# Hybrid encoder trunk, out-projection and first up chunk: GpSimd's sums and splits moved to VectorE, operands traced just ahead of their products, the token factors' transposes three products later

## The chip, the cores and the metric

The kernel runs on one core of a Trainium2 chip. The metric is the device time of one execution in microseconds; the time quoted is the median of several executions. TensorE multiplies matrices, VectorE and ScalarE work element by element, GpSimd is the fourth compute engine, SyncE issues most of the transfers. The engines run beside one another and wait for each other at semaphores.

## What is computed

Two layers. Each takes x (1024 tokens of 1024 features), mixes tokens in three parallel head groups, projects back and adds, and then runs a gated feed-forward network with a depthwise convolution of width 3 on the gate:

```python
mix = jnp.concatenate([o_a, o_b.astype(x.dtype), o_c], axis=-1)
x = x + mix @ w_out[l].astype(x.dtype)

hf = rms_norm(x, ffn_norm[l]) @ w_up[l].astype(x.dtype)
gate, val = hf[..., :D_FF], hf[..., D_FF:]
gate = depthwise_conv(gate, conv_w[l], conv_b[l])
x = x + (jax.nn.gelu(gate, approximate=False) * val) @ w_down[l].astype(x.dtype)
```

D_FF is 2816, everything is float32, and the norm is x · rsqrt(mean(x²) + eps) · gain over the features of a token.

## The kernel before

All data stand with features on the partitions and tokens along the row. A float32 product is made of three: each operand is split in a high half (a rounded copy, made by ScalarE) and a low half (the rest, a subtraction), and high·high, high·low and low·high are summed in PSUM. Every split thus costs a ScalarE copy and then a subtraction, on VectorE unless something else is said.

**Out-projection** (`out_proj`, L963 to L1006). A loop over the eight blocks of 128 output features, in the order 0, 4, 1, 5, 2, 6, 3, 7, here called columns. Each column takes 48 matmuls of 128x512 (L269). Then the old x is added (L983, VectorE), the sum `X` stored (L984), squared (ScalarE, L990) and added into a running sum of squares `ssq` (L991): on GpSimd, but for the last column on VectorE. The rest of the column already prepares the feed-forward: for blocks 0 to 3 the difference of the two token halves (`xd`, L997, GpSimd), scaled by the gain (L998), and the split of operand 11; for blocks 4 to 7 the second half of `xd` (L1004) and the split of operand T2. In the seventh column `up_begin` (L1080) traces the weights of the first up chunk.

**Up-projection** (`up`, L1083). 22 chunks, each 128 gate and 128 value features. A chunk is a 2x2 block product (halves of the 1024 inputs, halves of the tokens), made with seven block products instead of eight. `up_weights` loads a chunk's two weight blocks (L1051, L1052, on SyncE's queue) and makes seven weight operands of them (`wo`, splits L1063 and L1064). The seven token operands (`bo`) are the same for all chunks, made once a layer: 11, 21, T2, T1, T3, T4, 22, each of four pieces [high, low] of 128x512, made by `split_x` (L1011); T3 and T4 first need a scaled difference (`xt`, L1096 and L1097; `xd`, L1101). A product is twelve matmuls (L1111). In a chunk they come in the order 0 to 6 by the operands just listed, with product 0 of the next chunk (`begin`, L1122) between the fifth and the sixth. Product 0 and the later ones of a chunk add into one PSUM tile `pa`, and ScalarE copies its stages out: after product 0 (L1126), after T2 (L1139), after T3 (L1146).

**Token factors** (`factors`, L1023). The rsqrt factor of a token is applied behind the products. Eight products of `ssq` with a column of ones (L1028) sum over the features, VectorE and GpSimd make the rsqrt (L190, L195), eight transposes (L1036) spread it over the partitions, and two ScalarE copies (L1037) store it as `rbc`. All of that is called after product T2 of the first chunk.

**What sets the order.** A tile framework deals the traced instructions to each engine in an order of its own: by the order in which the code traces them, by what they wait for, and by its own model of times. Then each engine runs its row strictly in order. Buffers come from rings: 13 slots (`X`, `xd`, `sq`, `v`, `g`, operand 22), 16 for operands 21, T1, T3 and T4, 8 for 11 and T2, 10 for weights, 3 half-width ones (`xt`, one weight sum); PSUM has two tiles each of `pa`, `pb` and `pt`. An instruction that takes a ring's next buffer waits until its last reader is done, on whatever engine that is. In the code before, all of 21, T1, T3, T4 and 22 are traced ahead of product 0, and T1's four low halves are subtracted on GpSimd.

## Time and profile before

| what | value |
|---|---|
| median of 3 executions | 2807.78 us (2807.61 to 2809.55) |
| the profiled execution | 2816.99 us, span 2815.2 us |
| mean granted clock of TensorE | 0.991 of full |
| busy: TensorE, VectorE, ScalarE, GpSimd | 2760.4, 2146.6, 1431.8, 477.3 us |

The profile is of one execution. Its span starts with the first instruction on the device; times of the trace are counted from there. A matmul of 128x512 at the full clock starts 0.2267 us behind the one ahead of it; the trace's duration of a single one is longer, since matmuls overlap. [...] Layer 0's up-projection begins at 774.92, right behind the out-projection; layer 1's at 2171.44.

### The profile page before, as it was taken

Reading aid. Unit: us, or ns where it says so; the run is one execution under the profiler, and the core shown is the slowest. Engines: PE = TensorE matmul, PEld = TensorE weight load, DVE = VectorE, ACT = ScalarE, POOL = GpSimd, SP = SyncE. Lnnn points to the kernel's source line nnn. Section 1 sums busy time; section 2 is a strip of 40 time slices with the busy share of each in tenths; the row PEclk is TensorE's granted clock in tenths of the full one; section 3 lists DMA queues with packets and bytes.
Section 4 is the critical chain, followed back from the end, with each engine's and each line's share of the span. In section 5 each row is a group of like instructions: output and inputs, shape, how many; then the busy total and the mean of one; then the engine's idle time right before and its main releaser. Section 6 shows DMA issues by size and latency. Waiting matters only on the chain.

```text
span 2815.2 us, 39626 instructions
## 1 busy us (share of the span) xinstructions
PE 2760.4 (98%) x14984; PEld 2346.1 (83%) x14984; DVE 2146.6 (76%) x3330; ACT 1431.8 (51%) x2405; POOL 477.3 (17%) x349
## 2 busy tenths in 40 slices
PE   8999999999999999999999999999999999999999
PEld 7999987677878888888899999867778788888887
DVE  5858778798677777788848497788976778778885
ACT  5526367687353344344535264677864444334342
POOL 1202235442310000000002032354323000000000
PEclk9999999999999999999999999999999999999999
DMA  4313362010422222475313033521003122225661
GB/s 152 84 35 103 85 153 72 23 39 8 135 82 68 90 90 73 153 279 157 122 55 87 25 106 96 136 71 46 16 32 134 61 90 89 69 90 197 222 198 64
DMA packets 155200, 273.60 MB, mean 97 GB/s; under 512 B 16769, under 2 KB 74369, under 8 KB 155009
## 3 DMA queue, kind: packets, MB, share of 16 engines
q1 hardware_dynamic: 145216, 241.71, 26.4%
q0 software_dynamic: 9792, 29.36, 4.0%
q8 instruction: 118, 1.93, 0.3%
q14 instruction: 74, 0.60, 0.1%
HBM read 201.80 MB, written 69.21 MB: 96 GB/s over the span
## 4 chain that ended last, share of the span: by engine, by line
PE 87%; DVE 7%; ACT 3%; POOL 1%; issue 1%; DMA 1%; DVEq 0%; SPq 0%; ACTq 0%; POOLq 0%
PE pa L1111 17%; PE pa L281 11%; PE pa L269 11%; PE pb L1111 9%; PE pa L1309 6%; PE pb L860 5%; PE pa L774 5%; PE pt L1309 4%; PE pb L1309 4%; PE pt L1111 4%; PE pt L845 4%; PE pb L619 1%; PE pt L619 1%; DVE ptl L855 1%; PE pt L281 1%
## 5 line engine op out<-in xcount | busy, mean ns | idle before, releaser
L1111 PE MATMUL pa<-bo,wo 128*128 128x512 f32 x2112 | 505.4, 391 | 7.2 <-ACT v L1126 7.2
L1111 PEld LDWEIGHTS pa<-bo,wo 128*128 128x128 f32 x2112 | 398.9, 189 | 91.2 <-ACT v L1126 8.0
L281 PE MATMUL pa<-wh,xh 128*128 128x256 f32 (+1 forms) x864 | 263.6, 306 | 7.9 <-ACT xh L233 7.9
L774 PE MATMUL pa<-qk,qk 96*128 96x512 f32 (+1 forms) x896 | 257.8, 415 | 7.6 <-ACT pa L791 4.2
L281 PE MATMUL pa<-wl,xh 128*128 128x256 f32 (+1 forms) x864 | 262.5, 304 | 2.5 <-DVE wl L336 2.5
L281 PE MATMUL pa<-wh,xl 128*128 128x256 f32 (+1 forms) x864 | 261.4, 304 | 2.5 <-DVE xl L234 2.5
L1111 PE MATMUL pb<-bo,wo 128*128 128x512 f32 x1056 | 253.6, 389 | 0.0
L1111 PEld LDWEIGHTS pb<-bo,wo 128*128 128x128 f32 x1056 | 198.2, 188 | 41.2
L855 DVE TENSOR_TENSOR ptl<-pt,pth 128x512 fp32r<-128x512 f32 x240 | 162.1, 684 | 46.3 <-ACT pth L849 45.0
L1170 ACT ACTIVATE t<-g,pp 128x1024 f32<-128x1024 f32 x44 | 54.8, 1245 | 268.4 <-DVE g L1120 254.7
L774 PEld LDWEIGHTS pa<-qk,qk 96*128 96x128 f32 (+1 forms) x896 | 157.4, 191 | 38.3 <-ACT pa L791 5.1
L849 ACT ACTIVATE pth<-pt 128x512 fp32r<-128x512 f32 x256 | 149.2, 597 | 78.3 <-PE pt L845 74.1
L809 DVE CUSTOM_DVE_ANT_0 pb<-pa,toep 128x1024 f32<-128x1024 f32 x128 | 153.7, 1217 | 29.9 <-PE pa L774 29.5
L1309 PE MATMUL pa<-bw,bw 128*128 128x512 f32 x616 | 174.6, 389 | 0.0
L281 PEld LDWEIGHTS pa<-wh,xh 128*128 128x128 f32 x864 | 166.0, 192 | 8.1 <-ACT xh L233 7.9
L281 PEld LDWEIGHTS pa<-wl,xh 128*128 128x128 f32 x864 | 166.1, 192 | 3.2 <-DVE wl L336 3.0
L281 PEld LDWEIGHTS pa<-wh,xl 128*128 128x128 f32 x864 | 165.3, 192 | 3.4 <-DVE xl L234 3.1
L812 ACT ACTIVATE pb<-pb,nmb 128x1024 f32<-128x1024 f32 x128 | 147.1, 1151 | 36.6 <-DVE nmb L809 35.4
L1063 ACT ACTIVATE wo<-ws 128x512 fp32r<-128x512 f32 x176 | 102.4, 625 | 121.0 <-DVE ws L1059 107.9
L793 POOL TENSOR_SCALAR pa<-pa,z 128x1024 f32<-128x1024 f32 x96 | 110.4, 1150 | 157.8 <-PE pt L845 105.7
L1111 PE MATMUL pt<-bo,wo 128*128 128x512 f32 x528 | 134.7, 390 | 1.8 <-ACT wo L1063 1.8
L1309 PEld LDWEIGHTS pa<-bw,bw 128*128 128x128 f32 x616 | 115.6, 188 | 24.1
(310 smaller groups left out, 6394.2 us busy)
## 6 DMA issues: line engine op xcount, KB each, us to landing
wraw<-w_u SPq DMA_DIRECT2D x88, 512.0 KB, 4.3
hid<-t SPq DMA_DIRECT2D x44, 512.0 KB, 2.9
dq<-hid SPq DMA_DIRECT2D x66, 256.0 KB, 5.1
bk<-st SPq DMA_DIRECT2D x256, 48.0 KB, 1.7
qk<-bk POOLq DMA_DIRECT2D x32, 384.0 KB, 5.0
da<-w_d SPq DMA_DIRECT2D x44, 256.0 KB, 4.8
dp<-w_d SPq DMA_DIRECT2D x44, 256.0 KB, 5.4
dq<-w_d SPq DMA_DIRECT2D x44, 256.0 KB, 4.9
```

The lines of the kernel that those rows point to most:

```text
L269: nc.tensor.matmul(ps[:, hf * 512 : hf * 512 + 512], w, x[:, hf * 512 : hf * 512 + 512], start=first, stop=last)
L281: self.nc.tensor.matmul(ps, x[:, ts], w[:, k % kp, :cols], start=first, stop=last)
L774: nc.tensor.matmul(ps[:, hs], q[:rows, o + t * P : o + (t + 1) * P], kk[w][:rows, hs], start=w == 0, stop=w == 1)
L793: nc.gpsimd.tensor_scalar(e, e, z, 1.0, op0=ALU.mult, op1=ALU.mult)
L809: nc.vector.tensor_tensor_reduce(e, ps, self.toep[:, o : o + T], scale=-slope, scalar=3.0e38, op0=ALU.add, op1=ALU.min, accum_out=nm)
L812: nc.scalar.activation(e, e, AF.Exp, bias=nm, scale=-1.0, accum_out=z[:, t, i : i + 1])
L845: nc.tensor.transpose(ps[:, t * P : (t + 1) * P], Pt[t][:, k * P : (k + 1) * P], self.ident)
L849: nc.scalar.activation(hi[:, kk], ps, AF.Copy)
L855: nc.vector.tensor_tensor(lo[:, kk], ps, hi[:, kk], op=ALU.subtract)
L860: nc.tensor.matmul(acc, s, x, start=k == 0 and j == 0, stop=k == NT - 1 and j == len(ops) - 1)
L1111: nc.tensor.matmul(ps, st, mv, start=first and k + u + v == 0, stop=k == 3 and u == 1, skip_group_check=not first)
L1309: nc.tensor.matmul(acc[j][c], a[u][:, c * P : (c + 1) * P], b[v], start=g == first and q + u + v == 0, stop=q == n - 1 and u == 1, skip_gr ...
```

## The change

The six sums and four differences of a layer go from GpSimd to VectorE, T1's low halves too. The five later operands are traced by a function `build` that the first product of each calls, and T3 ahead of the first add of the chunk. In the first chunk, product 0 is copied to a half-width tile `u1`, and the slots `v` and `g` are taken later. `factors` ends with the rsqrt, and the transposes and copies, now `spread`, are called after product 0 of the second chunk, three products later; both use PSUM tiles `pt`.

```diff
@@ out_proj @@
-                (nc.vector if n == KC - 1 else nc.gpsimd).tensor_tensor(acc, acc, sq, op=ALU.add)
+                nc.vector.tensor_tensor(acc, acc, sq, op=ALU.add)
...
-                nc.gpsimd.tensor_tensor(d[:, 0], X[c][:, 512:], X[c][:, :512], op=ALU.subtract)
+                nc.vector.tensor_tensor(d[:, 0], X[c][:, 512:], X[c][:, :512], op=ALU.subtract)
@@ split_x @@
-            (eng or nc.vector).tensor_tensor(o[:, 1], src, o[:, 0], op=ALU.subtract)
+            nc.vector.tensor_tensor(o[:, 1], src, o[:, 0], op=ALU.subtract)
@@ factors @@
-        ps = self.bank1([P, NT])
+        ps = self.bank1([P, NT], tag="pt")
...
         self.rsqrt(r, ps, D, [NT])
+        return r
+
+    def spread(self, r):
+
+        nc = self.nc
         rbc = self.slot([P, T], name="rbc")
         for hf in range(2):
-            pb = self.bank1([P, 512])
+            pb = self.bank1([P, 512], tag="pt")
@@ up @@
-        for name in ("21", "T1", "T3", "T4", "22"):
+        def build(name):
+
...
-                    o = self.split_x(td[k][:, 0], None, self.xslot, nc.gpsimd)
+                    o = self.split_x(td[k][:, 0], None, self.xslot)
...
+            if (x, 0) not in self.B:
+                build(x)
...
-        def begin():
-
-            v, a = self.slot([P, T], name="v"), self.bank2([P, 512])
+        def begin(u1=None):
+
+
+            v = self.slot([P, T], name="v") if u1 is None else None
+            u1, a = v[:, :512] if u1 is None else u1, self.bank2([P, 512])
             product(0, "11", a)
-            nc.scalar.activation(v[:, :512], a, AF.Copy)
-            return v, a
+            nc.scalar.activation(u1, a, AF.Copy)
+            return v, u1, a
...
-        v, a = begin()
+        v, u1, a = begin(self.half([P, 512], "u1"))
...
-            g, c = self.slot([P, T], name="g"), self.bank1([P, 512], tag="pt")
+            c = self.bank1([P, 512], tag="pt")
             product(1, "21", c)
-            self.mark = [add(v[:, :512], v[:, :512], c)]
+            if f == 0:
+                build("T3")
+                v = self.slot([P, T], name="v")
+            self.mark = [add(v[:, :512], u1, c)]
...
-            if rbc is None:
-                rbc = self.factors(acc)
+            if f == 0:
+                r = self.factors(acc)
...
+            g = self.slot([P, T], name="g")
...
             coming = None if last else begin()
             self.ops = ops + self.ops
+            if f == 0:
+                rbc = self.spread(r)
```

The lines behind it move: the products are at L1118, the transposes at L1041, the copies after products 0, T2 and T3 at L1135, L1151 and L1159, the weight loads at L1056 and L1057, their splits at L1068 and L1069.

Layer 0, VectorE, from the add of the eighth column on. Before (`wo` is a weight of the second chunk; of the `bo`, 7897 is 21, 7915 to 7927 are T3, 7952 and 7955 are 22, 7885 is T2):

```order
L983 TENSOR_TENSOR X_7828<-X_7828,pa_7830 128x1024
L1064 TENSOR_TENSOR wo_7998<-wraw_7994,wo_7998 128x512
L1004 SCALAR_TENSOR_TENSOR xd_7822<-X_7828,pp,xd_7822 128x512
L991 TENSOR_TENSOR ssq_7389<-ssq_7389,sq_7881 128x1024
L1020 SCALAR_TENSOR_TENSOR bo_7897<-X_7828,pp,bo_7897 128x512
L1017 TENSOR_TENSOR bo_7915<-xt_7912,bo_7915 128x512
L1017 TENSOR_TENSOR bo_7921<-xt_7918,bo_7921 128x512
L1017 TENSOR_TENSOR bo_7927<-xt_7924,bo_7927 128x512
L1059 TENSOR_TENSOR ws_1393_8092<-wraw_7994,wraw_7993 128x512
L1059 TENSOR_TENSOR ws_7997<-wraw_7993 128x512
L1020 SCALAR_TENSOR_TENSOR bo_7952<-X_7403,pp,bo_7952 128x512
L1020 SCALAR_TENSOR_TENSOR bo_7955<-X_7537,pp,bo_7955 128x512
L1017 TENSOR_TENSOR bo_7885<-xd_7822,bo_7885 128x512
```

and in the changed kernel (`bo` 7913 is 21, 7885 T2, 7939 T3; `xd` at L1107 is T4's):

```order
L983 TENSOR_TENSOR X_7828<-X_7828,pa_7830 128x1024
L1069 TENSOR_TENSOR wo_7933<-wraw_7929,wo_7933 128x512
L1004 SCALAR_TENSOR_TENSOR xd_7822<-X_7828,pp,xd_7822 128x512
L1020 SCALAR_TENSOR_TENSOR bo_7913<-X_7828,pp,bo_7913 128x512
L1017 TENSOR_TENSOR bo_7885<-xd_7822,bo_7885 128x512
L1107 SCALAR_TENSOR_TENSOR xd_7822<-X_7828,pp,xd_7822 128x512
L1103 SCALAR_TENSOR_TENSOR xt_7936<-X_7403,pp,xt_7936 128x512
L1103 SCALAR_TENSOR_TENSOR xt_7942<-X_7537,pp,xt_7942 128x512
L1069 TENSOR_TENSOR wo_7974<-wraw_7929,wo_7974 128x512
L991 TENSOR_TENSOR ssq_7389<-ssq_7389,sq_7881 128x1024
L1017 TENSOR_TENSOR bo_7939<-xt_7936,bo_7939 128x512
L1064 TENSOR_TENSOR ws_7932<-wraw_7928 128x512
```

The last piece of T2 has come from the twelfth place behind the add to the fourth, and T3's differences, traced late, stand in front of the sum.

ScalarE at the same point, from the same weight of the second chunk on. Before (of the `bo`, 7900 is T1; the last row is the copy of product 0):

```order
L1063 ACTIVATE wo_7998<-wraw_7994 128x512
L990 ACTIVATE sq_7881<-X_7828 128x1024
L1019 ACTIVATE bo_7897<-X_7828,pp 128x512
L1016 ACTIVATE bo_7900<-xd_7391 128x512
...
L1019 ACTIVATE bo_7952<-X_7403,pp 128x512
L1019 ACTIVATE bo_7955<-X_7537,pp 128x512
L1016 ACTIVATE bo_7885<-xd_7822 128x512
L1063 ACTIVATE wo_8014<-wraw_7994 128x512
L1019 ACTIVATE bo_7958<-X_7671,pp 128x512
L1096 ACTIVATE xt_7930<-X_7735,pp 128x512
L1019 ACTIVATE bo_7961<-X_7828,pp 128x512
L1126 ACTIVATE v_7964<-pa_7965 128x512
```

and in the changed kernel, where the copy of product 0 writes `u`:

```order
L1068 ACTIVATE wo_7933<-wraw_7929 128x512
L1019 ACTIVATE bo_7913<-X_7828,pp 128x512
L1016 ACTIVATE bo_7885<-xd_7822 128x512
L1135 ACTIVATE u_1350_7888<-pa_7889 128x512
L1102 ACTIVATE xt_7936<-X_7336,pp 128x512
L1102 ACTIVATE xt_7942<-X_7469,pp 128x512
L1068 ACTIVATE wo_7974<-wraw_7929 128x512
L990 ACTIVATE sq_7881<-X_7828 128x1024
L1016 ACTIVATE bo_7939<-xt_7936 128x512
L1016 ACTIVATE bo_7945<-xt_7942 128x512
L1102 ACTIVATE xt_7948<-X_7603,pp 128x512
L1102 ACTIVATE xt_7954<-X_7735,pp 128x512
```

The copy of product 0 stands three places behind the weight's split instead of seventeen. The `xt` at 7948 and 7954 take half-width buffers that `xt` 7936 and 7942 have held, behind VectorE's `bo` 7939 and 7945.

TensorE from the sum over the features on. Before (7460 to 7885 are T2, 7915 T3, `pt` 8141 belongs to product 21 of the second chunk):

```order
L1111 MATMUL pt_8141<-bo_7888,wo_8014 128x512 x2
L1111 MATMUL pa_7965<-bo_7460,wo_7804 128x512 x3
L1111 MATMUL pa_7965<-bo_7594,wo_7804 128x512 x3
L1111 MATMUL pa_7965<-bo_7728,wo_7804 128x512 x3
L1111 MATMUL pa_7965<-bo_7885,wo_7804 128x512 x3
L1111 MATMUL pt_8141<-bo_7888,wo_8014 128x512
L1111 MATMUL pt_8141<-bo_7891,wo_8014 128x512 x3
L1111 MATMUL pt_8141<-bo_7894,wo_8014 128x512 x3
L1111 MATMUL pt_8141<-bo_7897,wo_8014 128x512 x3
L1036 MATMUL pb_8031<-ident,r_8027 128x128 x4
L1036 MATMUL pb_8037<-ident,r_8027 128x128 x4
L1111 MATMUL pa_7965<-bo_7915,wo_7812 128x512 x3
```

and in the changed kernel (7939 to 7957 are T3, 7991 is T1, `pb` 8179 is the second chunk's product of T1):

```order
L1118 MATMUL pa_7889<-bo_7728,wo_7804 128x512 x3
L1118 MATMUL pa_7889<-bo_7885,wo_7804 128x512 x3
L1028 MATMUL pt_7978<-ones,ssq_7389 128x1 x8
L1118 MATMUL pa_7889<-bo_7939,wo_7812 128x512 x3
L1118 MATMUL pa_7889<-bo_7945,wo_7812 128x512 x3
L1118 MATMUL pa_7889<-bo_7951,wo_7812 128x512
L1118 MATMUL pb_7990<-bo_7991,wo_7807 128x512
L1118 MATMUL pb_8179<-bo_7991,wo_8032 128x512
L1118 MATMUL pa_7889<-bo_7951,wo_7812 128x512 x2
L1118 MATMUL pa_7889<-bo_7957,wo_7812 128x512
L1041 MATMUL pt_8059<-ident,r_7987 128x128 x4
L1041 MATMUL pt_8065<-ident,r_7987 128x128 x4
```

T2 now stands ahead of the ones-products, T3 ahead of T1, with a few matmuls of T1 in it, and the transposes among them.

SyncE's queue keeps its order there. The last column's load of `X` waited for a GpSimd sum and now waits for VectorE's sum of the seventh column; the first weight load of the second chunk waits as before for VectorE's last split of the first chunk's weights, the second for a product of the last column; the first weight load of the third chunk waited for the first T4 split and now for the first split of 22.

In layer 1 the start of the attention is dealt differently too. VectorE, before (`st` are the copies that TensorE transposes, `va` and `v` the values):

```order
L467 TENSOR_TENSOR ass_15915<-ass_15915,fa 128x16
L468 TENSOR_TENSOR aqr_15806<-aqr_15806,ass_15915 128x1024
L725 TENSOR_TENSOR st_15925<-aqr_15635,st_15925 128x4x64 x2
L725 TENSOR_TENSOR st_15952<-aqr_15635,st_15952 128x4x64
L471 TENSOR_TENSOR asq_15805<-aqr_15806,rope 128x1024
L725 TENSOR_TENSOR st_15952<-aqr_15635,st_15952 128x4x64
L544 SCALAR_TENSOR_TENSOR va_16034<-pa_16039,r_12590,va_16034 128x64 x2
L546 SCALAR_TENSOR_TENSOR v_16035<-pa_16039,r_12590,v_16035 128x64
L547 SCALAR_TENSOR_TENSOR v_16035<-pa_16039,r_12590,v_16035 128x192
L546 SCALAR_TENSOR_TENSOR v_16035<-pa_16039,r_12590,v_16035 128x64
L547 SCALAR_TENSOR_TENSOR v_16035<-pa_16039,r_12590,v_16035 128x192
L472 TENSOR_TENSOR aqr_15806<-aqr_15806,rope 128x1024
```

and in the changed kernel:

```order
L467 TENSOR_TENSOR ass_15916<-ass_15916,fa 128x16
L468 TENSOR_TENSOR aqr_15807<-aqr_15807,ass_15916 128x1024
L544 SCALAR_TENSOR_TENSOR va_16035<-pa_16040,r_12591,va_16035 128x64 x2
L546 SCALAR_TENSOR_TENSOR v_16036<-pa_16040,r_12591,v_16036 128x64
L471 TENSOR_TENSOR asq_15806<-aqr_15807,rope 128x1024
L547 SCALAR_TENSOR_TENSOR v_16036<-pa_16040,r_12591,v_16036 128x192
L725 TENSOR_TENSOR st_15926<-aqr_15636,st_15926 128x4x64
L546 SCALAR_TENSOR_TENSOR v_16036<-pa_16040,r_12591,v_16036 128x64
L547 SCALAR_TENSOR_TENSOR v_16036<-pa_16040,r_12591,v_16036 128x192
L725 TENSOR_TENSOR st_15926<-aqr_15636,st_15926 128x4x64
L725 TENSOR_TENSOR st_15953<-aqr_15636,st_15953 128x4x64 x2
L472 TENSOR_TENSOR aqr_15807<-aqr_15807,rope 128x1024
```

The `st` copies have moved behind `va` and part of `v`. TensorE's order there has moved with it: groups of up to 16 products of the projection stand on the other side of some transposes (L729) and of the first score products (L774).

## Rows read from the trace of the kernel before

**Rows 1.** The profile's page, part 1: busy time of each engine over the whole span, its share, and the number of instructions.

```profile
PE 2760.4 (98%) x14984; PEld 2346.1 (83%) x14984; DVE 2146.6 (76%) x3330; ACT 1431.8 (51%) x2405; POOL 477.3 (17%) x349
```

**Rows 2.** The waits of TensorE over the whole span, by line and tile that waited and by engine, tile and line that released it: us in total, times, longest.

```profile
PE pa L1111 <- ACT v L1126: 7.2, 2, 3.6
...
PE pt L1111 <- ACT wo L1063: 1.8, 2, 0.9
```

**Rows 3.** TensorE's timeline in layer 0, from the first product of the first up chunk, and a batch of ones-products from the norm at the start of layer 1. Columns: start in us, time of the group, engine and line, operation, tile written and tiles read, shape, number, and in brackets the idle time in front of it with its releaser. The starts tell the pace; the times of groups overlap a little.

```profile
774.92 2.88 PE L1111 MATMUL pa<-bo,wo 128*128 128x512 f32 x12
...
785.83 0.73 PE L1111 MATMUL pt<-bo,wo 128*128 128x512 f32 x2 [0.90 <-ACT wo L1063]
790.14 4.99 PE L1111 MATMUL pa<-bo,wo 128*128 128x512 f32 x12 [3.58 <-ACT v L1126]
794.97 2.46 PE L1111 MATMUL pt<-bo,wo 128*128 128x512 f32 x10
797.27 1.03 PE L1036 MATMUL pb<-ident,r 128*128 128x128 f32 x8
798.06 3.01 PE L1111 MATMUL pa<-bo,wo 128*128 128x512 f32 x12
...
834.00 0.61 PE L1111 MATMUL pt<-bo,wo 128*128 128x512 f32 x2
...
853.04 0.62 PE L1111 MATMUL pt<-bo,wo 128*128 128x512 f32 x2
...
1428.31 1.84 PE L249 MATMUL pb<-ones,ssq 128*128 128x1 f32 x16
```

**Rows 4.** The same view of layer 1: the first product of its first up chunk, and the point of the rhythm that answers to 834.00.

```profile
2171.44 2.88 PE L1111 MATMUL pa<-bo,wo 128*128 128x512 f32 x12
...
2230.30 0.62 PE L1111 MATMUL pt<-bo,wo 128*128 128x512 f32 x2
```

**Rows 5.** Busy time in a stretch of 2 us, in this order: the stretch and its length, TensorE's matmuls, TensorE's weight loads, VectorE, ScalarE, GpSimd (each with its number of instructions), the mean granted clock of TensorE, the share of the DMA engines, and GB/s.

```profile
788.00:790.00 2.00, 0.00 (x0) 0.00 (x0) 2.00 (x4) 0.51 (x1) 0.00 (x0) 0.50 0.00 0
```

**Rows 6.** ScalarE's timeline in layer 0: the first weight split of the second up chunk, and the copy of product 0.

```profile
777.67 0.63 ACT L1063 ACTIVATE wo<-wraw 128x512 fp32r<-128x512 f32 x1 [7.26 <-DMA wraw<-w_u]
...
789.49 0.60 ACT L1126 ACTIVATE v<-pa 128x512 f32<-128x512 f32 x1 [1.88 <-DVE bo L1020]
```

**Rows 7.** VectorE's timeline in layer 0: the add of the seventh column and all that follows up to the eighth, and four later rows.

```profile
764.24 1.22 DVE L983 TENSOR_TENSOR X<-X,pa 128x1024 f32<-128x1024 f32 x1 [2.62 <-PE pa L269]
765.38 0.69 DVE L1064 TENSOR_TENSOR wo<-ws,wo 128x512 fp32r<-128x512 f32 x1
765.98 1.79 DVE L1064 TENSOR_TENSOR wo<-wraw,wo 128x512 fp32r<-128x512 f32 x1
767.69 4.22 DVE L1020 SCALAR_TENSOR_TENSOR bo<-X,pp,bo 128x512 fp32r<-128x512 f32 x3
771.83 0.74 DVE L1097 SCALAR_TENSOR_TENSOR xt<-X,pp,xt 128x512 f32<-128x512 f32 x1
772.49 0.74 DVE L1020 SCALAR_TENSOR_TENSOR bo<-X,pp,bo 128x512 fp32r<-128x512 f32 x1
773.15 0.68 DVE L1064 TENSOR_TENSOR wo<-ws,wo 128x512 fp32r<-128x512 f32 x1
...
778.34 0.69 DVE L1064 TENSOR_TENSOR wo<-wraw,wo 128x512 fp32r<-128x512 f32 x1 [1.94 <-ACT wo L1063]
...
782.51 5.09 DVE L1017 TENSOR_TENSOR bo<-xt,bo 128x512 fp32r<-128x512 f32 x3
...
790.04 0.68 DVE L1017 TENSOR_TENSOR bo<-xd,bo 128x512 fp32r<-128x512 f32 x1
```

**Rows 8.** GpSimd's timeline in the same stretch: the difference and the sum of the seventh column, and T1's four splits.

```profile
765.54 1.68 POOL L997 TENSOR_TENSOR xd<-X 128x512 f32<-128x512 f32 x1 [7.11 <-DVE X L983]
767.58 2.46 POOL L991 TENSOR_TENSOR ssq<-ssq,sq 128x1024 f32<-128x1024 f32 x1 [0.36 <-ACT sq L990]
780.47 6.58 POOL L1017 TENSOR_TENSOR bo<-xd,bo 128x512 fp32r<-128x512 f32 x4 [10.43 <-ACT bo L1016]
```

**Rows 9.** SyncE's queue: the issue of the two weight loads for the second up chunk of layer 0.

```profile
773.90 0.33 SPq L1051 DMA_DIRECT2D wraw<-w_u  x1
774.66 0.33 SPq L1052 DMA_DIRECT2D wraw<-w_u  x1
```

**Rows 10.** DMA issues between 740 and 800: tiles, queue, number, KB each, median us from issue to landing.

```profile
X<-xT SPq DMA_DIRECT2D x3, 512.0 KB, 4.4
```

**Rows 11.** The waits of TensorE between 1735 and 1835, in the first part of layer 1's attention; the longest first.

```profile
PE pb L914 <- POOL obrs L911: 0.4, 1, 0.4
```

**Rows 12.** TensorE's timeline at two other waits: a transpose of layer 0's projection stage, and score products of layer 1's attention.

```profile
326.19 0.54 PE L729 MATMUL pt<-identr,st 128*128 128x128 f32 x4 [2.19 <-DVE st L725]
...
1889.27 1.40 PE L774 MATMUL pa<-qk,qk 96*128 96x512 f32 x4 [1.61 <-DVE nmb L809]
```

**Rows 13.** Busy time in stretches behind the idle times and the ones-products above; the columns are those of Rows 5, the clock is the third number from the end.

```profile
1890.00:1892.00 2.00, 2.00 (x5) 1.11 (x5) 1.93 (x6) 1.68 (x4) 0.00 (x0) 0.52 0.02 6
...
326.00:328.00 2.00, 1.80 (x13) 1.80 (x13) 1.40 (x5) 2.00 (x6) 0.53 (x1) 0.69 0.82 215
...
332.00:334.00 2.00, 2.00 (x13) 2.00 (x13) 0.45 (x3) 1.03 (x3) 1.46 (x1) 0.60 0.00 0
...
1430.00:1432.00 2.00, 2.00 (x18) 2.00 (x18) 0.17 (x1) 0.00 (x0) 1.56 (x1) 1.00 0.00 0
```

More of the change, by code (lines that the diff above doesn't have):

```diff
@@ L1160, in up @@
             if not last:
-                v, a = coming
+                v, u1, a = coming
     def gate(self, l, f, g, rbc):
```

3 lines of the change are left out of this document (1 added, 2 removed).

## Prediction

> **What bounds the kernel now.** TensorE is busy 98% of the span [rows 1], so only time in which it waits, or runs at the lower clock, can be won. The waits of TensorE, grouped by line and releaser, name the place: the products of the first up chunk (L1111) wait 7.2 us in two waits for a ScalarE copy `v`, and 1.8 us in two for a split weight `wo` [rows 2]: one of each per layer. Then I read that stretch as a timeline. From the first product at 774.92 to 834.00, where the next chunks repeat, there are 218 matmuls of 128x512 [rows 3]. The steady rhythm is 84 of them in 19.04 us (834.00 to 853.04), 0.2267 us each. 218 × 0.2267 = 49.42; the stretch took 59.08, a loss of 9.66 us. The same in layer 1: 2171.44 to 2230.30 is 58.86, a loss of 9.44 [rows 4]. The parts of it in layer 0: the ones-products some 1.84 (such a batch stands undisturbed at 1428.31 in the layer's first norm), idle 0.90 and 3.58, 0.28 in the two matmuls at 785.83 (4.31 to the next row, less 3.58 and 0.45), twelve matmuls from 790.14 to 794.97 in 4.83 instead of 2.72 (2.11 lost), the transposes 0.79, and 0.16 in small pieces [rows 3]. The 2.11 is the clock: 0.50 in 788 to 790, the lower of the two levels [rows 5]; from 794.97 on the matmuls have their full pace again.
>
> Why was `v` late? ScalarE's copy at 789.49 had itself waited for VectorE's low half of a split (L1020) [rows 6]: the copy stood behind the operands of T1, T3 and 22 on ScalarE's queue, and these wait for buffers that VectorE frees. VectorE is the slow one: busy all of that stretch [rows 5], and it lost time beside GpSimd. Three splits at 782.51 took 5.09 us, 1.70 each, while GpSimd ran its four; one at 790.04, with GpSimd idle, took 0.68 [rows 7, 8].
>
> **The change, part by part.** I take VectorE's steps (start to start) from rows without GpSimd: 1.14 us for a 128x1024 (764.24 to 765.38), 0.66 for a scalar-tensor-tensor of 128x512 (771.83 to 772.49), 0.60 for a tensor-tensor of 128x512 (765.38 to 765.98) [rows 7].
>
> *Sums and differences on VectorE.* Six sums (1.14) and four differences (0.60) a layer are 9.2 us more for VectorE. In the columns this is covered: a column is 48 matmuls, 10.88 us, and VectorE sat idle 2.62 us in front of the add at 764.24, waiting for TensorE [rows 7]. If that cover were gone, the next column's weights would come late; it isn't, as the next point shows. The last column decides. VectorE's row of work there began at 764.24 and ended with the split at 773.15 plus 0.68, at 773.83: 9.6 us, though its pieces alone are 1.14 + 3 × 0.60 + 5 × 0.66 = 6.24. The 3.3 us between lie beside GpSimd's difference at 765.54 and sum at 767.58 [rows 7, 8]. After: one scalar-tensor-tensor goes (an `xt`, now traced later), a difference and a sum come, 6.24 - 0.66 + 0.60 + 1.14 = 7.32, and the row ends at 771.64, 2.2 us sooner, in spite of the added work.
>
> That matters, since SyncE's load of the next chunk's first weight was issued at 773.90, just when that last split had ended, and its buffer is what it waited for [rows 9]. ScalarE waited for it 7.26 us, until 777.67 [rows 6], some 3.7 behind the issue. It would be issued near 771.7 and land near 775.4. What else it waits for, a product of the third-last column and an old transfer, is long over. The second load waits for the last column's products and stays at 774.66. One load comes later: the last column's `X`, ahead of these on SyncE's queue, now waits for VectorE's sixth sum, which ends at 769.7; 4.4 us under way [rows 10], it lands near 774.2, one microsecond ahead of the add at 775.17. So VectorE's row of work behind the last add can start with the weight's low half at 776.4, where it was 778.34 [rows 7].
>
> *Operands just ahead of products.* The order shows what stands there now: weight, `xd`, operand 21, T2's split fourth (it was twelfth), T4's `xd`, two `xt`, a weight, the sum, and T3's four operands among first-chunk work; T1, T4 and 22 come behind. ScalarE's copy of product 0 stands three places behind that weight instead of seventeen. From 776.37 to the low half of T3's third operand there are eleven tensor-tensors (6.60), seven scalar-tensor-tensors (4.62), the sum 1.14, the rsqrt start 0.07, and some 0.35 of waits for ScalarE: it starts at 789.15 and is done at 789.83. TensorE wants it after 57 matmuls and the ones-products: 774.92 + 12.92 + 1.75 = 789.59. So a wait of 0.1 to 0.2 us is left. T2's operand is done near 779.1 (the fourth step) and read after 45 matmuls, at 785.1, so the wait of 3.58 goes, and with it the 0.90 (the second chunk's product 21, which waited for its weight, no longer stands there). A new wait: two of T3's `xt` need the half-width buffers that `u1` and the first two `xt` hold, so ScalarE stops until VectorE's first two T3 splits end, near 783.6 and 784.8 (776.37 and the ten steps up to the first, 6.84, with 0.4 of waits; two more steps for the second); behind it is queued the copy of T2's product, which ends only at 785.8 (48 matmuls). Covered.
>
> *T1's splits on VectorE.* Four times 0.60, behind T3's operands. Each T1 operand feeds six matmuls, 1.36 us, so 0.60 apart is fast enough; covered. The next pair of weight loads now waits for two splits of operand 22, VectorE's thirteenth and fifteenth steps behind T3's third split: near 797 and 798.5, half a chunk (19.04) ahead of the products that read them; covered.
>
> *Transposes later.* The factor chain is a VectorE step, GpSimd's power and eight transposes; three products later it has time. In layer 1 I allow 0.26 for a factor that comes that late. The ones (1.75) and transposes (0.79) themselves stay on TensorE.
>
> What remains: 1.75 + 0.79 + 0.15 and small pieces of 0.15 make 2.84 in layer 0 and 3.10 in layer 1. Gain 9.66 - 2.84 = 6.8 and 9.44 - 3.10 = 6.3, **13.1 us**. Nothing else moves in layer 0. In layer 1 the scheduler also deals the start of the attention differently (copies `st` behind `va` and `v`); TensorE's largest wait in 1735 to 1835 is 0.4 us [rows 11], so nothing is to be won and I take 0, with 3 us either way. The sums go by the profiled execution (2816.99 us, span 2815.2), which is 9.2 above the median of the runs; as differences they are set against the median, 2807.78.
>
> [...]
>
> **The rivals.** *First: the early load gains nothing* (it and the `X` load ahead of it slow each other, and it lands at 777.6). Then the third T3 operand is done at 791.83, TensorE waits 2.2 us in pieces, and 4.8 + 4.35 = 9.2 is won: 2798.6. For it: the load was 3.7 us under way beside a second one; against: what else it waits for is over long before. *Second: the clock falls as well.* An idle of 2.19 at 326.19 and one of 1.61 at 1889.27 were followed by a mean clock of 0.69 and 0.52, ones-products of 1.84 us without idle at 1428.31 were not [rows 3, 12, 13]. With 2.2 us idle beside the ones, twelve matmuls could again run at half speed, 1.7 each layer: 9.2 - 3.4, 2802. [...] *Third: VectorE becomes the bound,* its 1.70 not being GpSimd's doing. Then the last column ends at 774.9, the load lands 1.1 later than before, the T3 splits stay 1.0 longer each: 2.3 + 1.1 + 3.1 = 6.5 waited, 0.6 won a layer, 2806.6. Against it: each slow VectorE row read has a GpSimd row across it. *Fourth, slower: layer 1's dealt-over attention start.* There `st` copies that TensorE's transposes (L729) read now stand behind `va` and `v`, which wait for a projection's products and for ScalarE. If a transpose waits as one did at 326.19, it costs 2.19 [rows 12] and half of the time at the lower clock behind it: 1.24 us of 326 to 328 by the mean of 0.69, 1.6 of 332 to 334 by 0.60, and the four between [rows 13], 6.8 in all; so 5.6. Three such waits, 16.8, less 13.1: 2811.5. It decides from the third wait on; one alone gives 2800.3. Against: this stage has few waits now.
>
> **How the numbers follow.** Forecast 2794.7, 0.58; first rival 0.17; second 0.08; third 0.06; fourth 0.04 (and 0.07 for one or two such waits or other mishaps, in the same stage). The forecast's own range, with 3 us for the order in layer 1, is 2791.5 to 2798; the first two rivals take it up to 2802. A run of this kernel can tell about 0.2%, 5.6 us: faster means under 2802.2. Forecast, first rival and half of the mishaps and of the second rival: 0.82; slower 0.04; the rest 0.14.
>
> **What would show it.** Right: no wait of L1118 products for `v` over 0.5 us; the clock at full from 786 on; the first weight load of the second chunk issued near 771.7; VectorE's L1017 at 0.68 throughout; TensorE's stretch from the first product to the start of the third chunk's repeat at 52 to 53 us. Wrong: waits of 1 us at T3's third operand with the load still at 773.9 (first rival), the clock at 0.50 after the ones (second), L1017 over 1 us with GpSimd idle (third), new waits at L729 or L774 in layer 1 (fourth).

## The result, and the profile after

The changed kernel is slower: 2815.63 us, median of 13 executions (2812.05 to 2817.88), against 2807.78 for 13 of the kernel before; ratio 1.0024, 95% interval 1.0017 to 1.0031. Forecast were 2794.7 us and a range of 2791.5 to 2802: wrong in sign and size. The profiled execution took 2815.45 us. One execution of e5_stop (3416 us) and one of e10_gpsimd_only (3045 us), both below, ran at a mean granted clock of 0.75 and 0.85, and the ratios there leave them out. The page's busy times, against [rows 1]: TensorE is still at 98%, GpSimd has 45 us less to do.

```profile
PE 2755.1 (98%) x14984; PEld 2341.3 (83%) x14984; DVE 2133.4 (76%) x3358; ACT 1431.5 (51%) x2405; POOL 432.6 (15%) x321
```

The waits of TensorE over the whole span (us in total, times, longest), against [rows 2]:

```profile
PE pt L1041 <- POOL r L195: 14.4, 2, 7.2
```

The waits for `v` and `wo` are gone from the first chunk, as forecast. In their place the transposes of the token factors wait 7.2 us in each layer, for GpSimd's power. TensorE's timeline in layer 0, against [rows 3]; the last row is the point of the rhythm that answers to 834.00 there:

```profile
767.61 2.88 PE L1118 MATMUL pa<-bo,wo 128*128 128x512 f32 x12
...
778.49 1.84 PE L1028 MATMUL pt<-ones,ssq 128*128 128x1 f32 x16
780.19 1.88 PE L1118 MATMUL pa<-bo,wo 128*128 128x512 f32 x7
781.97 0.73 PE L1118 MATMUL pb<-bo,wo 128*128 128x512 f32 x2
782.66 0.97 PE L1118 MATMUL pa<-bo,wo 128*128 128x512 f32 x3
790.82 1.97 PE L1041 MATMUL pt<-ident,r 128*128 128x128 f32 x8 [7.19 <-POOL r L195]
792.43 1.20 PE L1118 MATMUL pa<-bo,wo 128*128 128x512 f32 x2
793.43 6.68 PE L1118 MATMUL pb<-bo,wo 128*128 128x512 f32 x22
...
830.33 0.62 PE L1118 MATMUL pt<-bo,wo 128*128 128x512 f32 x2
```

The order is the forecast's, and up to 782.66 no row has a wait. Then the transposes come, the queue is strict, and behind them stand 24 matmuls that wait only for their turn: here they start 24.82 us behind the first product, and in e4_late, below, with the transposes out of the way, 16.42 us behind it, with no wait of more than 0.23. From the first product to 218 matmuls on it is 62.72 us; before it was 59.08. Layer 1, against [rows 4]: 61.25 us, before 58.86.

```profile
2166.51 2.88 PE L1118 MATMUL pa<-bo,wo 128*128 128x512 f32 x12
...
2189.46 1.97 PE L1041 MATMUL pt<-ident,r 128*128 128x128 f32 x8 [7.20 <-POOL r L195]
...
2227.76 0.62 PE L1118 MATMUL pt<-bo,wo 128*128 128x512 f32 x2
```

That is 3.64 + 2.39 = 6.0 of the 7.85 us between the medians; where the rest lies was not followed. The clock follows the wait; windows of layer 0 (columns as in [rows 5], the granted clock third from the end):

```profile
786.00:788.00 2.00, 0.00 (x0) 0.00 (x0) 2.00 (x5) 0.07 (x1) 2.00 (x1) 0.60 0.00 0
788.00:796.00 8.00, 5.18 (x17) 4.41 (x18) 1.23 (x3) 2.33 (x5) 2.76 (x1) 0.50 0.00 0
796.00:798.00 2.00, 2.00 (x9) 1.66 (x8) 1.36 (x2) 2.00 (x5) 0.00 (x0) 0.84 0.00 0
```

Windows of 0.25 us read 1.00 up to 786.25, 0.50 from 786.50 to 796.50 and 1.00 again from 796.75. In the trace before, too, such windows read 1.00 or 0.50 from 786 to 798 and from 325 to 337, but for the four in which it changes (0.66, 0.69, 0.56 and 0.79); these are the two levels that the forecast reckons with. Here it falls to 0.50 while TensorE stands still, and part of the 22 matmuls after the transposes run at it: 6.52 us from their start to the next row (799.95), where 22 at full pace take 4.99.

Why is the power late? GpSimd's timeline has one instruction in this stretch of each layer; between them stands the same instruction in the norm at the start of layer 1, with VectorE idle:

```profile
781.49 9.28 POOL L195 TENSOR_TENSOR r<-r,mhalf 128x8 f32<-128x8 f32 x1 [112.33 <-DVE r L190]
...
1426.83 1.64 POOL L195 TENSOR_TENSOR r<-r,mhalf 128x8 f32<-128x8 f32 x1 [636.07 <-DVE r L190]
...
2180.13 9.27 POOL L195 TENSOR_TENSOR r<-r,mhalf 128x8 f32<-128x8 f32 x1 [112.04 <-DVE r L190]
```

GpSimd had nothing else to do, its input was there, and a power over 128x8 took 9.28 us. VectorE's timeline, against [rows 7]:

```profile
756.93 1.22 DVE L983 TENSOR_TENSOR X<-X,pa 128x1024 f32<-128x1024 f32 x1 [3.85 <-PE pa L269]
...
763.66 0.69 DVE L1069 TENSOR_TENSOR wo<-ws,wo 128x512 fp32r<-128x512 f32 x1
...
781.25 0.15 DVE L190 TENSOR_SCALAR r<-pt 128x8 f32<-128x8 f32 x1
781.32 0.68 DVE L1069 TENSOR_TENSOR wo<-ws,wo 128x512 fp32r<-128x512 f32 x1
...
783.73 4.90 DVE L1017 TENSOR_TENSOR bo<-xd,bo 128x512 fp32r<-128x512 f32 x8
788.54 0.68 DVE L1069 TENSOR_TENSOR wo<-ws,wo 128x512 fp32r<-128x512 f32 x1
796.28 0.69 DVE L1069 TENSOR_TENSOR wo<-wraw,wo 128x512 fp32r<-128x512 f32 x1 [7.05 <-ACT wo L1068]
```

From 781.32 to 789.22 VectorE runs thirteen tensor-tensors with both operands in SBUF, one straight behind the other. The power starts inside that row and ends at 790.77, 1.55 behind its end: about as long as the undisturbed one takes (1.64). So it looks as though the power could not begin until VectorE's row was over. The kernel before had this, too, in a place that I had not read: GpSimd and VectorE in layer 0's attention, and at the factors themselves,

```profile
222.06 5.84 POOL L195 TENSOR_TENSOR css<-css,mhalf 128x8 f32<-128x8 f32 x1 [1.65 <-DVE bss L497]
...
792.08 2.11 POOL L195 TENSOR_TENSOR r<-r,mhalf 128x8 f32<-128x8 f32 x1 [5.04 <-DVE r L190]
```

```profile
225.46 0.94 DVE L498 TENSOR_TENSOR bqk<-bqk,bss 128x768 f32<-128x768 f32 x1
227.94 0.69 DVE L689 TENSOR_TENSOR co<-pb,css 128x512 f32<-128x512 f32 x1 [1.53 <-POOL css L195]
...
792.58 0.74 DVE L1097 SCALAR_TENSOR_TENSOR xt<-X,pp,xt 128x512 f32<-128x512 f32 x1
```

The power at 222.06 ended at 227.90, 1.50 behind VectorE's last tensor-tensor (226.40). The one at 792.08, among scalar-tensor-tensors, took 2.11, and ended 1.61 behind the start of the one at 792.58.

### The profile page after: what moved, and what is told of

It is laid out like the page before. It is cut to its first block, busy times and chain, and to the rows that moved or that the text cites. A ratio compares the mean times of both kernels' runs of the same rounds, so it can differ in the third digit from the quotient of the medians.

```text
span 2813.7 us, 39594 instructions
## 1 busy us (share of the span) xinstructions
PE 2755.1 (98%) x14984; PEld 2341.3 (83%) x14984; DVE 2133.4 (76%) x3358; ACT 1431.5 (51%) x2405; POOL 432.6 (15%) x321
## 4 chain that ended last, share of the span: by engine, by line
PE 82%; DVE 7%; issue 5%; ACT 2%; POOL 2%; DMA 1%; POOLq 0%; SPq 0%; DVEq 0%; ACTq 0%
PE pa L1118 16%; PE pa L281 11%; PE pb L1118 8%; PE pa L269 7%; PE pa L1324 6%; PE pb L860 5%; PE pa L774 5%; PE pt L1324 4%; PE pb L1324 4%; PE pt L1118 4%; PE pt L845 3%; PE pb L619 1%; PE pt L619 1%; PE pt L281 1%; DVE ptl L855 1%
## 5 line engine op out<-in xcount | busy, mean ns | idle before, releaser
L1118 PE MATMUL pa<-bo,wo 128*128 128x512 f32 x2112 | 503.4, 390 | 0.0
L1118 PEld LDWEIGHTS pa<-bo,wo 128*128 128x128 f32 x2112 | 396.6, 188 | 82.4 <-DVE bo L1017 0.6
L774 PE MATMUL pa<-qk,qk 96*128 96x512 f32 (+1 forms) x896 | 256.3, 412 | 5.4 <-DVE nmb L809 3.2
L1118 PE MATMUL pb<-bo,wo 128*128 128x512 f32 x1056 | 255.7, 391 | 0.0
L1118 PEld LDWEIGHTS pb<-bo,wo 128*128 128x128 f32 x1056 | 199.7, 189 | 42.3 <-ACT bo L1016 0.6
L774 PEld LDWEIGHTS pa<-qk,qk 96*128 96x128 f32 (+1 forms) x896 | 156.5, 190 | 35.4 <-DVE nmb L809 4.8
L1068 ACT ACTIVATE wo<-ws 128x512 fp32r<-128x512 f32 x176 | 102.2, 625 | 119.5 <-DVE ws L1064 106.0
L195 POOL TENSOR_TENSOR r<-r,mhalf 128x8 f32<-128x8 f32 x4 | 21.8, 5459 | 871.9 <-DVE r L190 871.9
L1118 PE MATMUL pt<-bo,wo 128*128 128x512 f32 x528 | 134.3, 389 | 0.0
```

The costliest lines, as they stand in the source:

```text
L774: nc.tensor.matmul(ps[:, hs], q[:rows, o + t * P : o + (t + 1) * P], kk[w][:rows, hs], start=w == 0, stop=w == 1)
L1068: nc.scalar.activation(o[:, 0], src, AF.Copy)
L1118: nc.tensor.matmul(ps, st, mv, start=first and k + u + v == 0, stop=k == 3 and u == 1, skip_group_check=not first)
```

## The experiments

The theory, **"VectorE's unbroken row keeps the power out"**, with as its first rival that GpSimd, idle for 112 us, is slow to take up a power again; the expectations call the two 'port' and 'cold', which are names of mine: no run here shows a port. Each kernel below is the changed one but for its edit, unless something else is said. "Stretch" is the time from the first product to 218 matmuls later, layer 0 / layer 1; every median is set against runs of the kernel before on the same chip.

**e1_warm.** A throwaway power on GpSimd in the seventh column, some 20 us ahead of the real one:

```
             if n == KC - 2:
+                wm = self.small([P, NT], name="wm", bufs=2)
+                nc.gpsimd.tensor_tensor(wm, sq[:, :NT], self.mhalf[:, :NT], op=ALU.pow)
```

> The changed kernel, and besides GpSimd makes one throwaway power of 128x8 in the seventh column of each layer, some 15 us ahead of the one that counts. [...] Rival 'cold': the power is slow because GpSimd had run nothing for 112 us and had to fetch its code; then the throwaway one takes the 9.3, the real one 1.6 to 2.1, the waits go, and the median is near 2797.

GpSimd's timeline in layer 0:

```profile
762.32 1.94 POOL L994 TENSOR_TENSOR wm<-sq,mhalf 128x8 f32<-128x8 f32 x1 [91.01 <-ACT sq L990]
783.49 9.24 POOL L195 TENSOR_TENSOR r<-r,mhalf 128x8 f32<-128x8 f32 x1 [19.23 <-DVE r L190]
```

The throwaway one, after 91 us of idleness, took 1.94; the real one 9.24 as ever, 19.23 us behind it. Median 2816.25, ratio 1.0019 (1.0010 to 1.0029). The idle engine is not the cause, and a fetch of code no run shows.

**e3_stt.** The low halves of T1 to T4 as scalar-tensor-tensors, with a multiplication by one, of the same size and with the same two operands in SBUF:

```
-            nc.vector.tensor_tensor(o[:, 1], src, o[:, 0], op=ALU.subtract)
+            nc.vector.scalar_tensor_tensor(o[:, 1], src, self.ones[:, 0:1], o[:, 0], op0=ALU.mult, op1=ALU.subtract)
```

> The changed kernel with the low halves of T1, T2, T3 and T4 written as scalar-tensor-tensor (times one, minus the high half) in place of tensor-tensor; the order on VectorE stays. In the kernel before, the power of 2.11 us ran beside a row of scalar-tensor-tensor steps. Theory 'port': at the border between two of these GpSimd gets in, as there; tensor-tensors of weights stand among them up to 2.5 us behind the power's start, so the power takes 2.1 to 4.5 us, TensorE waits under 2.5 us for it, and the median falls to 2798 to 2803. [...] Rival 'cold': 9.3, median 2816.

The timeline of all engines around the power:

```profile
782.58 0.68 DVE L1069 TENSOR_TENSOR wo<-ws,wo 128x512 fp32r<-128x512 f32 x1
782.74 2.05 POOL L195 TENSOR_TENSOR r<-r,mhalf 128x8 f32<-128x8 f32 x1 [112.61 <-DVE r L190]
783.18 0.75 DVE L1017 SCALAR_TENSOR_TENSOR bo<-xt,ones,bo 128x512 fp32r<-128x512 f32 x1
```

The power took 2.05 and ended at 784.79, 1.61 behind the start of the first scalar-tensor-tensor, though VectorE never paused. No wait for it is left; stretch 53.01 / 52.79, median 2799.73, ratio 0.9967 (0.9956 to 0.9978). VectorE's work is the same or a little more (0.66 a step for 0.60), and the loss is gone.

**e4_late.** The power left as slow as it is, the transposes held behind the last matmul of T4 in the first chunk:

```
-                    nc.tensor.matmul(
+                    mm = nc.tensor.matmul(
...
+            return mm
...
+            mm = product(5, "T4", a, False)
             if f == 0:
-                rbc = self.spread(r)
-            product(5, "T4", a, False)
+                with self.tc.issue_after(mm.ins):
+                    rbc = self.spread(r)
```

> The changed kernel with the transposes pinned on TensorE behind the last matmul of product T4 of the first chunk, 42 matmuls or 9.5 us later; nothing else. Both theories: the power stays slow (8 to 10 us), but TensorE has other work meanwhile, so its waits of 7.2 us and the half clock behind them go. If the rest of the prediction was right, the stretch from the first product to the rhythm point is 52 to 53.5 us in both layers (62.7 and 61.3 in the changed kernel), median 2796 to 2799. If instead T1's and T4's operands on VectorE are too late for TensorE, waits of 1 us or more appear at products of T1 or T4 and the median stays over 2802.

GpSimd's timeline, then TensorE's, then VectorE's:

```profile
782.19 9.88 POOL L195 TENSOR_TENSOR r<-r,mhalf 128x8 f32<-128x8 f32 x1 [112.48 <-DVE r L190]
```

```profile
784.56 0.73 PE L1118 MATMUL pa<-bo,wo 128*128 128x512 f32 x2 [0.23 <-DVE bo L1017]
```

```profile
790.45 0.68 DVE L1128 TENSOR_TENSOR g<-g,pb 128x512 f32<-128x512 f32 x1
```

The power is no faster, but now TensorE does not wait for it: stretch 53.44 / 53.34, median 2797.13, ratio 0.9951 (0.9934 to 0.9967). So what costs the time is that the transposes stand ahead of work that is ready.

**e5_stop.** VectorE made to wait for the power, ahead of T1's low halves, by a copy of its result:

```
-            product(3, "T1", b)
+            if f == 0:
+                r2 = self.small([P, NT], name="rc", bufs=2)
+                cp = nc.vector.tensor_copy(r2, r)
+                with self.tc.issue_after(cp.ins):
+                    product(3, "T1", b)
+                r = r2
+            else:
+                product(3, "T1", b)
```

> The changed kernel with a VectorE copy of the power's result, behind which T1's and T4's low halves are queued, so that VectorE itself stops for the power after T3's last split; the transposes read the copy. Theory 'port': the power ends 1.5 to 1.7 us after VectorE's last T3 split and takes 3.5 to 5 us in all; TensorE waits 1 to 3 us instead of 7.2, median 2799 to 2804. Rival 'cold': the power takes 9.3 us whatever VectorE does, and VectorE's splits are later as well: median 2818 or more.

VectorE's timeline:

```profile
781.54 0.68 DVE L1017 TENSOR_TENSOR bo<-xt,bo 128x512 fp32r<-128x512 f32 x1
783.79 0.17 DVE L1157 COPY rc<-r 128x8 f32<-128x8 f32 x1 [1.57 <-POOL r L195]
```

Standing still for 1.57 us, VectorE let the power through in 2.05 (781.71 to 783.76). That is better than expected: the engines' orders are dealt anew as well, and only one tensor-tensor now stands between the rsqrt start and the stop, so that TensorE does not wait for the power at all. Stretch 52.16 / 52.16, the shortest of all; median 2797.70, ratio 0.9955 (0.9941 to 0.9969). With an added wait on a busy engine the kernel is some 18 us faster than the changed one by the medians (which were set against other runs of the kernel before: 2809.88 here, 2807.78 there).

**e6_one.** Only the one low half right behind VectorE's rsqrt start is a scalar-tensor-tensor (the traced weight `wo` at 781.32 above):

```
-        def split(src):
+        def split(src, one=False):
...
+            if one:
+                nc.vector.scalar_tensor_tensor(o[:, 1], src, self.ones[:, 0:1], o[:, 0], op0=ALU.mult, op1=ALU.subtract)
...
-        yield split(s[:, 0])
+        yield split(s[:, 0], f == 1)
```

> The changed kernel with one instruction a layer written otherwise: the low half of the second chunk's fourth weight operand as a scalar-tensor-tensor (times one, minus the high half) in place of a tensor-tensor. It stands directly behind the rsqrt's first step on VectorE, where the power becomes ready. Theory 'port': GpSimd gets in at the border in front of that one instruction, the power takes 1.7 to 2.1 us instead of 9.3, TensorE's waits of 7.2 us go, the stretch from the first product to the rhythm point is 52 to 53.5 us (62.7 and 61.3 in the changed kernel), median 2796 to 2799. Rival: one border is not enough, it takes a row of such instructions: 9 us again, 2815.

VectorE's timeline, then GpSimd's:

```profile
782.36 0.74 DVE L1070 SCALAR_TENSOR_TENSOR wo<-ws,ones,wo 128x512 fp32r<-128x512 f32 x1
783.02 0.68 DVE L1017 TENSOR_TENSOR bo<-xt,bo 128x512 fp32r<-128x512 f32 x1
```

```profile
782.53 9.33 POOL L195 TENSOR_TENSOR r<-r,mhalf 128x8 f32<-128x8 f32 x1 [112.54 <-DVE r L190]
```

What the theory expected did not come: 9.33, stretch 61.60 / 61.32, median 2816.10, ratio 1.0023 (1.0012 to 1.0033). The rows say why: this row had started at 782.36, 0.17 before the power, and the power did not get in while it ran, nor where the next tensor-tensor followed it at 783.02. In e3 it was let in at the border from a tensor-tensor to a scalar-tensor-tensor (783.18 there, 2.05 in all). So the theory needed a refinement, taken from these two runs: what counts is the instruction that VectorE begins when the power stands ready.

**e11_one_later.** The test of that: one scalar-tensor-tensor only, one place later on VectorE (`k == 2`, T3's third operand):

```
+            if one:
+                nc.vector.scalar_tensor_tensor(o[:, 1], src, self.ones[:, 0:1], o[:, 0], op0=ALU.mult, op1=ALU.subtract)
...
-                    o = self.split_x(d, None, self.xslot)
+                    o = self.split_x(d, None, self.xslot, k == 2)
```

> One low half only is a scalar-tensor-tensor, this time the fourth one traced (bo_7951, a column's third operand), so that VectorE has a border between a plain two-operand row and such a row only after the power has long been ready. Theory 'VectorE's unbroken row keeps the power out': the power enters at that one border and takes 1.9 to 2.3 us, no wait of TensorE for it is above 0.5 us, 218 matmuls from the first product take 52 to 54 us in both layers, and the median is 2796 to 2800. Rival 'one border is not enough': the power takes 9 us or more, TensorE waits 7 us for it in both layers, and the median is 2813 to 2818.

VectorE's timeline, then GpSimd's:

```profile
783.57 0.68 DVE L1072 TENSOR_TENSOR wo<-ws,wo 128x512 fp32r<-128x512 f32 x1
784.17 0.74 DVE L1018 SCALAR_TENSOR_TENSOR bo<-xt,ones,bo 128x512 fp32r<-128x512 f32 x1
```

```profile
783.74 2.05 POOL L195 TENSOR_TENSOR r<-r,mhalf 128x8 f32<-128x8 f32 x1 [112.47 <-DVE r L190]
```

One border was enough: 2.05, over at 785.79, again 1.62 behind it. No wait for the power; stretch 52.92 / 52.50, median 2798.64, ratio 0.9953 (0.9936 to 0.9970). One instruction of thirteen, changed in form and not in work, is worth 17 us against the changed kernel by the medians.

The last runs take the change apart. **e7_sums_back** is e4_late with the sums (but the last column's) and the differences on GpSimd again:

```
-                nc.vector.tensor_tensor(acc, acc, sq, op=ALU.add)
+                (nc.vector if n == KC - 1 else nc.gpsimd).tensor_tensor(acc, acc, sq, op=ALU.add)
...
-                nc.vector.tensor_tensor(d[:, 0], X[c][:, 512:], X[c][:, :512], op=ALU.subtract)
+                nc.gpsimd.tensor_tensor(d[:, 0], X[c][:, 512:], X[c][:, :512], op=ALU.subtract)
```

> The kernel with the transposes pinned behind product T4, and the six sums and four differences of a layer back on GpSimd; VectorE's order is otherwise the same. What the prediction says of them: VectorE's work in the last column ends 2.2 us later, so the second chunk's first weight is loaded 2.2 us later and VectorE's row of work behind it starts 1.9 us later; T3's third operand is late by 1.5 to 2.2 us, the stretch grows from 53.4 to 55 to 56 us in each layer, median 2800 to 2802. If the columns have slack enough for GpSimd: 53.4 and 2797 as before.

Stretch 54.50 / 54.45, 1.1 longer in each layer than e4_late, where more was expected; median 2801.34, ratio 0.9969 (0.9956 to 0.9981). The first weight load of the second chunk is issued 1.62 ahead of the first product; in the changed kernel 3.20 ahead.

**e9_trace_only** is e7_sums_back with T1's low halves on GpSimd as well, so that only the tracing and the held transposes remain of the change:

```
-                    o = self.split_x(td[k][:, 0], None, self.xslot)
+                    o = self.split_x(td[k][:, 0], None, self.xslot, nc.gpsimd)
```

> As the kernel with the transposes pinned behind T4, but with all of the GpSimd part undone: sums, differences and T1's low halves on GpSimd. Only the tracing and the transposes are changed against the kernel before. Beside the 2 us of the later load, T1's four GpSimd splits (1.65 each) lie across VectorE's T3 and weight splits, each of which they lengthen by about 1.0, and T1's operands come later: stretch 56 to 59 us, median 2802 to 2808, that is, most of the gain gone. Rival: order alone makes the gain, stretch under 54.5 us and median under 2799.

TensorE's timeline in layer 0, then GpSimd's, then VectorE's:

```profile
785.96 5.49 PE L1118 MATMUL pb<-bo,wo 128*128 128x512 f32 x12 [2.50 <-POOL bo L1017]
```

```profile
780.35 3.86 POOL L195 TENSOR_TENSOR r<-r,mhalf 128x8 f32<-128x8 f32 x1 [19.93 <-DVE r L190]
784.19 6.79 POOL L1017 TENSOR_TENSOR bo<-xd,bo 128x512 fp32r<-128x512 f32 x4
```

```profile
786.38 1.76 DVE L1069 TENSOR_TENSOR wo<-ws,wo 128x512 fp32r<-128x512 f32 x1
```

Stretch 59.91 / 59.38, longer than the 56 to 59 expected; median 2807.75, ratio 0.9998 (0.9984 to 1.0011): nothing won. T1's splits queue behind the power, take 1.70 each, and slow VectorE's rows beside them from 0.68 to 1.76.

**e10_gpsimd_only** is the kernel before with only the sums, the differences and T1's low halves on VectorE; the tracing and the transposes are as before:

```
-                    o = self.split_x(td[k][:, 0], None, self.xslot, nc.gpsimd)
+                    o = self.split_x(td[k][:, 0], None, self.xslot)
```

and the sums and differences as in the diff of the change.

> The kernel before with only the GpSimd part of the change: sums, differences and T1's low halves on VectorE, tracing and transposes as they were. The load comes 2.2 us earlier (VectorE's row 1.9), T1's splits cost VectorE 2.4 us ahead of T3's, three T3 splits last 1.8 us instead of 5.1: the copy of product 0 comes some 2.8 us sooner, the wait of 3.58 falls to about 0.8, and the clock stays up or falls for less: 2.8 to 4.9 us won a layer, median 2798 to 2802.5. The power stands there in front of scalar-tensor-tensors and stays near 2. Rival: VectorE is only more loaded, wait 3.5 or more, median 2808 or above.

TensorE's timeline in layer 0, then GpSimd's:

```profile
779.63 4.61 PE L1111 MATMUL pa<-bo,wo 128*128 128x512 f32 x12 [1.10 <-ACT v L1126]
```

```profile
781.68 2.10 POOL L195 TENSOR_TENSOR r<-r,mhalf 128x8 f32<-128x8 f32 x1 [112.17 <-DVE r L190]
```

The wait for `v` falls from 3.58 [rows 3] to 1.10, though the twelve matmuls behind it still take 4.45 us up to the next row (784.08), where the first twelve (767.94 to 770.66) take 2.72. The power finds scalar-tensor-tensors behind VectorE's rsqrt start, as before, and takes 2.10. Stretch 55.16 / 55.06, median 2801.64, ratio 0.9970 (0.9958 to 0.9981): this part alone wins 3.9 us a layer.

**e0_before** is the kernel before, once more, since the profile used for the forecast has its first product at 774.92 and all changed ones have theirs at 765 to 770.

> The kernel before, unchanged, for another profile of it. If the late first product (774.92) in the profile that the prediction used was that execution's own attention stage, this one has it at 767 to 770 us, the 218 matmuls from there take 58.8 to 59.3 us in layer 0 and 58.6 to 59.1 in layer 1, and the execution takes 2805 to 2812. If it belongs to the kernel, the first product starts at 774 to 776 again.

One execution, 2820.22 us: first product at 770.81, stretch 59.12 / 58.89. The stretches held; the start lies just outside what was expected and the time above it. The later start lies in the attention, where TensorE's timelines of the profile before and of this one show the same wait in different layers:

```profile
531.88 2.08 PE L774 MATMUL pa<-qk,qk 128*128 128x512 f32 x4 [2.94 <-ACT pa L791]
```

```profile
1931.06 2.08 PE L774 MATMUL pa<-qk,qk 128*128 128x512 f32 x4 [2.93 <-ACT pa L791]
```

In layer 0 the profile before runs 2.29 us ahead of this one before that wait (score products at 526.70 and 528.99) and 2.98 behind after it (539.63 and 536.65). A wait of this length stands there in one execution and not in the other; its origin was not followed. It lies outside the stretch, so the forecast's sums by stretches do not depend on it.

## Why the prediction was wrong

**The step that failed** is *Transposes later*: "The factor chain is a VectorE step, GpSimd's power and eight transposes; three products later it has time." Neither half of it held. It gave the power no price of its own, with only 0.26 us allowed in layer 1; the price was 9.28 and 9.27 us. And the transposes are three products later in the code alone: the framework dealt them on TensorE's queue behind 60 matmuls of the up-projection, as many as before (counted in TensorE's timelines), and twelve behind the ones-products where there had been 24. The two orders of TensorE in *The change* show the twelve and the 24, and the prediction did not count them. So the transposes stood five matmuls of T3 and T1 behind the power's start, and nearly all of what exceeds 2 us became idle time: 7.19 and 7.20 us. Behind that came the lower clock, 0.50 in 788 to 796: the eight transposes 0.82 longer than their forecast 0.79 (790.82 to 792.43), the two matmuls behind them 0.55 longer, and the 22 of layer 0 1.53. Together 10.1 us in layer 0 and, with 0.32 for the 22, 8.9 in layer 1: 19.0 of the 20.9 us between forecast and measurement. The rest, 1.9 us, is less than 0.1%, and I had said that 0.2% is what a measurement can tell. Where the transposes really stand later, by 42 matmuls (e4_late), a still slower power costs nothing.

The change made the starvation itself. The tracing put tensor-tensors (weights, T3) straight behind the rsqrt start, where scalar-tensor-tensors had stood (792.58 above); T1's low halves, moved to VectorE, made that row longer; and the transposes, no later on TensorE's queue than before, were not behind its end. Without the tracing the power takes 2.10 (e10_gpsimd_only); with T1's low halves back on GpSimd 3.86 (e9_trace_only), ending 1.54 behind a VectorE row that is over at 782.67; with the row as it is but the transposes behind it, its 9.88 cost nothing (e4_late). The sums have no part in it: e7_sums_back has them on GpSimd, and GpSimd's timeline shows the power at 9.88 there too.

```profile
783.02 9.88 POOL L195 TENSOR_TENSOR r<-r,mhalf 128x8 f32<-128x8 f32 x1 [19.93 <-DVE r L190]
```

**What was right.** Take those 10.1 and 8.9 away and the stretches are 52.6 and 52.3 us, the 52 to 53 that was forecast; e3_stt, e5_stop and e11_one_later, which free the power, measured 52.2 to 53.0, and medians of 2797.70 to 2799.73, inside the range forecast for the change and 10 to 12 us under the runs of the kernel before that they are set against, where 13.1 was forecast. By the steps:

- *The sums and differences on VectorE shorten its row in the last column.* (The forecast calls the seventh column so, whose add is the first row of it.) From that add at 756.93 to the last split's end at 764.35 (763.66 + 0.69) are 7.42 us, forecast 7.40 (764.24 to 771.64); before 9.6.
- *The weight load goes out 2.2 us earlier.* SyncE's queue, against [rows 9]:

```profile
764.41 0.33 SPq L1056 DMA_DIRECT2D wraw<-w_u  x1
```

  3.20 us ahead of the first product instead of 1.02: 2.18 earlier. The first ScalarE row that waits for it starts at 768.53, 0.92 behind the first product (before 2.75 behind [rows 6]). So the first rival, that the early load gains nothing, did not happen.
- *VectorE's splits at 0.68 without GpSimd.* L1017 runs at 0.60 a step (783.73: eight in 4.90). The third rival falls, and e9_trace_only shows the cause from the other side: with T1 back on GpSimd the rows beside it take 1.76.
- *No wait for `v` over 0.5 us; ones-products without a fall of the clock.* Both held up to the power: TensorE's waits from 767 to 835 have none for `v`, and the granted clock is 1.00 in every window of 2 us from 768 to 786. The second rival, the clock, came true only as a consequence of the new wait, with another cause than its own.
- *Layer 1's attention order.* TensorE's largest wait between 1735 and 1835 is the one that stood there before, 0.4 us [rows 11], and the fourth rival, which I had put on the slower side, did not happen. The slower side needed a different mechanism, which none of my four rivals had.

What each part is worth: GpSimd's work moved alone, 3.9 us a layer; the tracing alone, with the transposes held late, nothing measurable; together, with the power freed or the transposes held late, 5.6 to 6.9 in layer 0 (e4_late 53.44, e5_stop 52.16, against 59.08). The parts need each other: the tracing makes T1 urgent, and with T1's low halves on GpSimd TensorE waits 2.50 us for them (e9_trace_only).

**Why I did not see it.** I took the power's time from one row, the one beside it in the stretch, and had concluded from the splits that GpSimd slows VectorE; I never asked what VectorE does to GpSimd. Read together, the instances of L195 in the trace before show 1.64 to 5.84 us for the same 128x8, and what differs in those read here is what VectorE was running when each began. The row beside it alone does not decide: GpSimd and VectorE, still in the trace before,

```profile
1740.73 1.64 POOL L195 TENSOR_TENSOR css<-css,mhalf 128x8 f32<-128x8 f32 x1 [2.07 <-DVE ass L467]
```

```profile
1740.77 1.25 DVE L468 TENSOR_TENSOR aqr<-aqr,ass 128x1024 f32<-128x1024 f32 x1
```

show a power that began 0.04 ahead of such a tensor-tensor and was not held up. The one at 1740.73 was first and took 1.64; the one at 781.49 was second and ended 1.55 behind the last of thirteen such rows, so VectorE's next tensor-tensor went ahead of it at every border of that run. That the tensor-tensors had two operands in SBUF does not by itself tell which rows shut the power out: the scalar-tensor-tensors of e3_stt and e11_one_later had two as well, and the power ended 1.61 and 1.62 behind the start of one; in e10_gpsimd_only, too, it ended 1.61 behind the start of one (782.17).

## What to carry to other kernels

A small instruction on GpSimd had no fixed price here, 1.64 to 9.88 us for the same 128x8: look up every instance of it in the trace, and beside each what its neighbour engine ran. When a change packs an engine's row tighter, list who was living in the gaps of that row; the work that was moved away here made room, and the room was then filled by rows that shut GpSimd out (9.28 us for its power). And place an instruction that waits for such a chain (here eight transposes) behind work that is ready, since their wait, here 7.19 us, held up the 24 ready matmuls behind them as well; whether it stands there, the engine's own order tells, and not the order of the code.
